# A two-layer transformer block: earlier stack loads, one weight ring for all stages, other bytes for raw weights, later stores

## The chip, the cores and the metric

The kernel runs on one core of a Trainium2 chip. The metric is the device time of one execution in microseconds (us). Five engines work side by side, each through its own instructions in order: PE (TensorE) multiplies matrices, DVE (VectorE) and ACT (ScalarE) do elementwise work, POOL (GpSimd) does elementwise work and issues DMAs, SP (SyncE) issues DMAs only. They wait for each other by semaphores.

## The reference

Two layers over 1024 latent tokens and 256 context tokens of width 1024. Each layer norms and modulates the tokens, projects them, runs four mixers side by side, adds their projected output, and ends in a gated feed-forward. All of it is float32.

```
for l in range(DEPTH):                                  # DEPTH = 2
    need_ctx = l < DEPTH - 1
    u_lat = modulate(rms_norm(h, norm1_g[l]), sh1, sc1)
    u_ctx = modulate(rms_norm(hc, norm1_g[l]), csh1, csc1)
    y_lat, y_ctx = hybrid_mixer(u_lat, u_ctx, ...)      # mLSTM | attention | pooling | convolution
    h = h + g1 * (y_lat @ w_out[l])
    h = h + g2 * swiglu(modulate(rms_norm(h, norm2_g[l]), sh2, sc2), ffn_w_in[l], ffn_w_out[l])
    if need_ctx:
        hc = hc + cg1 * (y_ctx @ w_out[l])
        hc = hc + cg2 * swiglu(modulate(rms_norm(hc, norm2_g[l]), csh2, csc2), ffn_w_in[l], ffn_w_out[l])

def diff_softmax_attend(q, k, v, lam):                  # 4 heads, two maps m each
    s = jnp.einsum('bqhmd,bkhmd->bhmqk', q, k) * (A_HD ** -0.5)
    p = jax.nn.softmax(s, axis=-1)
    a = p[:, :, 0] - lam * p[:, :, 1]
    return jnp.einsum('bhqk,bkhe->bqhe', a, v)

def swiglu(u, w_in, w_out):
    g, up = jnp.split(u @ w_in, 2, axis=-1)
    return (jax.nn.silu(g) * up) @ w_out
```

The mLSTM is a recurrence over chunks of tokens, forward and backward.

## The kernel before

**Precision.** Each float32 operand is split into a high part and a rest (names ending in h and l; ACT copies the high part, DVE or POOL subtracts it), and each product is three matmuls: high by high, low by high, high by low (`mm3`).

**Stages of a layer.** A: norm, projections, mLSTM, convolution, pooling (`mixers`, line 612). B: attention (line 1171). C: output projection `out_proj` and the second norm (`norm_ffn`), lines 1412 and 1454. F: `ffn_in` (line 1536), in Strassen's form: 11 pairs of feature tiles by two halves x (gate, up), so 22 phases; in each, four loaded weights A11 to A22 and four sums S1 to S4 of them (POOL, lines 1552 to 1555) give seven products of 12 matmuls per part of the tokens; in layer 0 the context's products lie between them. G: `ffn_out`. In layer 0 the span is A 0 to 555, B to 870, C to 985, F to 1590, G to 1935; in layer 1 A ends at 2346, B near 2640, C at 2706, F at 3160.

**Memory.** Tiles come from pools with a number of buffers per tag; a new tile waits until the last reader of the buffer's former tile is done. A stage's pools are closed at its end, and the next stage's pools lie on their bytes, with the same kind of wait per tile. U: 16 big tiles that hold the normed projection input (uh, ul, two tiles for each of 8), later attention's stacks. S: 12 tiles of the same size for the mLSTM. The weight ring (`load_w`, line 299: tags wh, wl with 5 buffers, raw wr with 2) belongs to stages A to C; stage F has its own tags fr (raw weights), fh, fl (their split), ft (temporaries), and there the context's h is loaded into fr buffers, too (line 1519).

**Attention's input.** q and k are normed, rotated and written by POOL's queue to a DRAM tensor qks (line 991). `stacks(h)` (line 1184) loads head h from there, again by POOL's queue: for each of two maps m two copies of the rows of Qs and one Ks, into U tiles. The scores sc are matmuls of Ks by Qs.

**Order.** The Tile framework's scheduler places the instructions of each engine by priority in the order written, up to the attention; in attention PE, ACT and DVE are kept in the order written. In the mLSTM's loop the projections of attention's q, k and v and the convolution are interleaved by hand: `nfill` units of the generator `fill` are spread over the loop's 22 steps, and what is left of it runs behind the loop.

```
        steps = 2 * (len(self.oc) + 1)
        nfill = 24 if need else 20
```

Of the kernel before, what the change touches and what calls it, by code (L numbers as in the profile page):

```python
# [18 lines left out]
P = 128  # L19
D = 1024  # L20
KT = 8
# [163 lines left out]
class Builder:  # L185
    def __init__(self, tc, a, ctx):
        self.tc, self.a = tc, a
        self.ordered = False
        self.nc = Ordered(self, tc.nc)
        e = ctx.enter_context  # L190
        self.cp = e(tc.tile_pool(name="cp", bufs=1))
        self.qp = e(tc.tile_pool(name="qp", bufs=12))
        self.ps = None
        self.npool = 0
        self.dp = e(tc.tile_pool(name="dp", bufs=1, space=bass.MemoryType.DRAM))


# [9 lines left out]
    def open_mixers(self):  # L207
        self.mx = ExitStack()
        self.wx = ExitStack()
        self.wp = self.mkpool(self.wx, "right")  # L210
        self.tp = self.mkpool(self.mx, "left")
        self.sp = self.mkpool(self.mx, "left")
        self.mp = self.mkpool(self.mx, "left")
        self.temps = (self.tp, TW, 11)

    def E(self, tag, bufs, dt=F32, n=512):
        return self.fp.tile([P, n], dt, tag=tag, name=tag, bufs=bufs)

    def stage(self, temps=None):

        if self.fx is not None:
            self.fx.close()
        if temps:
            if self.tx is not None:
                self.tx.close()
            self.tx = ExitStack()
            self.temps = (self.mkpool(self.tx, "right"), 512, temps)
        self.fx = ExitStack()
        self.fp = self.mkpool(self.fx, "right")

# [381 lines left out]
    def mixers(self, l, u, norm, early_out):  # L612
# [102 lines left out]
        steps = 2 * (len(self.oc) + 1)  # L715
        nfill = 24 if need else 20
        done = step = 0
# [9 lines left out]
        for c in list(self.oc) + [None]:  # L727
            if old:
                next(old)
            if c is not None:  # L730
                new = self.mlstm_chunk(c, kT, qT, Cst)
                next(new)
            background()
            if old:
                next(old)
            if c is not None:
                next(new)
            background()
            old = new
        for _ in fill:  # L740
            pass
# [363 lines left out]
    def conv(self, acc):  # L1105
# [61 lines left out]
        for _ in range(5):  # L1167
            if next(self.rest):
                yield

    def attention(self, early):

        nc, l = self.nc, self.l
        ident = self.c("ident")
        ya = [self.S(f"ya{i}") for i in range(2)]
        gd = nc.gpsimd.dma_start

        def dup(ap):
            return AP(tensor=ap.tensor, offset=ap.offset, ap=[[0, 2]] + [list(x) for x in ap.ap])
        q0 = 0 if self.need else NCTX  # L1180
        els = [self.mp.tile([P, 2, NCH], F32, name="el", tag="el", bufs=2) for _ in range(2)]
        heads = {}

        def stacks(h):
            Qs, Ks = [], []
            for m in range(2):
                mp = 2 * h + m
                Qm = self.U(f"Qs{m}", F32R)
                for x in range(2):
                    gd(Qm[x * 64:x * 64 + 64, q0:NT].bitcast(F32), dup(self.qk_scr[0, mp, x, :, q0:NT].bitcast(F32)))  # L1190
                Km = self.U(f"Ks{m}", F32R)
                self.stack = gd(Km[:, 0:NT].bitcast(F32),
                                dup(self.qk_scr[1, mp].rearrange("a r n -> (a r) n").bitcast(F32)))
                Qs.append(Qm)
                Ks.append(Km)
            V = self.U("V")[:, :NCH * 64].rearrange("p (c x) -> p c x", x=64)
            nc.sync.dma_start(V, self.v_scr[h])
            heads[h] = (Qs, Ks, V)

        def scores(h, b0, nk, at):  # L1200
# [3 lines left out]
            for qb in range(2):  # L1204
# [3 lines left out]
                sums = (L0, ls[:, 3:4])  # L1208
                pr = [self.S(f"pr{m}") for m in range(2)]
                for m in range(2):  # L1210
# [52 lines left out]
        def values(h, b0, nk, aT):  # L1263
# [4 lines left out]
            for kt in range(nk):  # L1268
# [4 lines left out]
                if kt == nk // 2 - 1:  # L1273
                    yield
            yield
            for b in range(2):
                self.copy(ya[h // 2][rows, b0 + b * P:b0 + (b + 1) * P], po[b * 64:b * 64 + 64, 0:P])
# [65 lines left out]
        for k in range(max(plan) + 1):  # L1343
            if k == 0:
                stacks(0)
            if k % (4 * len(nblk)) == 2 and k // (4 * len(nblk)) < 3:
                stacks(k // (4 * len(nblk)) + 1)
            ev = plan.get(k, [])
# [63 lines left out]
    def out_proj(self, l, src, dst, chunks, later):  # L1412
# [5 lines left out]
        for i, (c0, n) in enumerate(chunks):  # L1418
# [12 lines left out]
            for nt in range(KT):  # L1431
# [7 lines left out]
                nc.vector.scalar_tensor_tensor(hv, ps[:, :n], self.mod[l][:, 16 + nt, v:v + 1], hv, ALU.mult, ALU.add)  # L1439
                nc.sync.dma_start(dst[nt][:, cs], hv)  # L1440
                for _ in range(3):
                    next(todo, None)
                if squares and nt:
                    squares.send(h[nt - 1])
            if i == 0:
                self.ux.close()
# [7 lines left out]
    def norm_ffn(self, l, need):  # L1454
# [58 lines left out]
        def ctx(src):  # L1513

            n = NCTX
            t = [self.E("uc", KT, F32R) for _ in range(KT)]
            h = [self.E("fr", 8)[:, :n] for _ in range(KT)]
            for k in range(KT):
# [17 lines left out]
    def ffn_in(self, l, state, mid, need, side):  # L1536
# [7 lines left out]
        def weights(f, x):  # L1544
            raw = {}
            for i, (ff, pc) in enumerate(((f, 0), (f, 1), (f + 1, 0), (f + 1, 1))):
                raw[i] = self.E("fr", 8 + 3 * more)
                nc.sync.dma_start(raw[i], self.a["ffn_in"][l, ff, x, pc])
            for i in (self.S1, self.S2, self.S3, self.S4):
                raw[i] = self.E("fr", 8 + 3 * more)  # L1550
            A11, A12, A21, A22, S1, S2, S3, S4 = range(8)
            gp(raw[S1], raw[A21], raw[A22], ALU.add)
            gp(raw[S2], raw[S1], raw[A11], ALU.subtract)
            gp(raw[S3], raw[A11], raw[A21], ALU.subtract)
            gp(raw[S4], raw[A12], raw[S2], ALU.subtract)
            return raw

        def split(raw):
            hi, lo = self.E("fh", 5 + 2 * more, F32R), self.E("fl", 5 + 2 * more, F32R)
            self.copy(hi, raw)  # L1560
            self.sub_lo(lo, raw, hi)
            return hi, lo
# [140 lines left out]
    def run(self):  # L1703
        nc, a = self.nc, self.a
        self.fx = self.tx = None
        self.open_u()
# [16 lines left out]
        for l in range(DEPTH):  # L1723
# [8 lines left out]
            self.phase("C")  # L1732
            self.stage(4)
            mid = self.dp.tile([KT, P, NT], F32, name=f"hmid{l}")
            state, norm = self.norm_ffn(l, need)
            self.out_proj(l, src, mid, ch, norm)
            self.phase("F")
            self.fx.close()
            self.tx.close()
            self.wx.close()  # L1740
            self.fx = self.tx = None
# [3 lines left out]
            self.phase("G")  # L1745
            self.stage()
            if need:
# [10 lines left out]
            later = iter(())  # L1758
            self.fx.close()
            self.tx.close()  # L1760
            self.fx = self.tx = None
            if need:
# [83 lines left out]
```

## Time and profile before

| | |
|---|---|
| three runs | 3417.82, 3414.29, 3411.08 us (median 3414.29) |
| the profiled execution | 3415.06 us, its span 3413.3 us |
| PE busy | 3020.0 us, 88% |
| DVE, ACT, POOL busy | 1935.9, 1318.5, 846.8 us |
| mean granted clock of PE | 0.939 of full speed |
| moved by DMA | 393.37 MB |

Times in the profile are microseconds from the span's start. A row of instructions names line, engine, operation, output<-input. All of PE, ACT and DVE stand under line 165, through which a helper records them; so groups are told apart by their tiles: tmps are projections, pS, pi and pN the mLSTM's matmuls, sc attention's scores, ops the output projection, nps a norm's sums, fps the feed-forward's products, fcs the same of the context. A waits row gives what an engine waited for, the sum, how often, and the longest. PEclk is the granted clock, 1.00 for 2.4 GHz and 0.50 for 1.2 GHz.

### The profile page before, as it was taken

Reading aid. Unit: us, or ns where it says so; the run is one execution under the profiler, and the core shown is the slowest. Engines: PE = TensorE matmul, PEld = TensorE weight load, DVE = VectorE, ACT = ScalarE, POOL = GpSimd, SP = SyncE. Lnnn points to the kernel's source line nnn. Section 1 sums busy time; section 2 is a strip of 40 time slices with the busy share of each in tenths; the row PEclk is TensorE's granted clock in tenths of the full one; section 3 lists DMA queues with packets and bytes.
Section 4 is the critical chain, followed back from the end, with each engine's and each line's share of the span. In section 5 each row is a group of like instructions: output and inputs, shape, how many; then the busy total and the mean of one; then the engine's idle time right before and its main releaser. Section 6 shows DMA issues by size and latency. Waiting matters only on the chain. (4 is left out here: it accounts for less than half of the span.)

```text
span 3413.3 us, 44185 instructions
## 1 busy us (share of the span) xinstructions
PE 3020.0 (88%) x16144; PEld 2399.7 (70%) x16144; DVE 1935.9 (57%) x3023; ACT 1318.5 (39%) x2605; POOL 846.8 (25%) x650
## 2 busy tenths in 40 slices
PE   7999885788978999999999798985879699999999
PEld 3767664556656888887887686764656478888787
DVE  6494565884447666763345559554882554544333
ACT  4212444774333222223334522433873433332322
POOL 2240321322223323321000224231322244433000
PEclk9999987988988999999999899987989899999999
DMA  7122334124743333333544411234226323221653
GB/s 269 55 73 98 94 87 97 42 62 167 239 132 115 121 111 118 117 112 116 176 170 165 132 41 47 74 104 87 58 56 237 123 93 98 75 86 50 208 171 134
DMA packets 295578, 393.37 MB, mean 115 GB/s; under 512 B 70720, under 2 KB 140480, under 8 KB 295360
## 3 DMA queue, kind: packets, MB, share of 16 engines
q1 hardware_dynamic: 251392, 360.47, 32.7%
q0 software_dynamic: 43968, 30.07, 4.7%
q8 instruction: 127, 2.08, 0.3%
q14 instruction: 91, 0.75, 0.1%
HBM read 304.28 MB, written 85.98 MB: 114 GB/s over the span
## 5 line engine op out<-in xcount | busy, mean ns | idle before, releaser
L165 PE MATMUL fps<-Uh,fh 128*128 128x512 f32 (+1 forms) x1288 | 495.8, 385 | 51.5 <-ACT fh L165 38.4
L165 PE MATMUL fps<-Uh,fl 128*128 128x512 f32 (+1 forms) x1288 | 493.7, 384 | 0.9 <-DVE fl L165 0.9
L165 PE MATMUL fps<-Ul,fh 128*128 128x512 f32 (+1 forms) x1288 | 494.2, 384 | 0.0
L165 ACT ACTIVATE fh<-fr 128x512 fp32r<-128x512 f32 x330 | 207.1, 631 | 543.7 <-PE fps L165 386.1
L165 DVE TENSOR_TENSOR fl<-fr,fh 128x512 fp32r<-128x512 f32 x330 | 269.7, 819 | 137.0 <-ACT fh L165 131.5
L165 PE MATMUL xps<-gl,xh 128*128 128x512 f32 (+1 forms) x880 | 327.2, 372 | 12.0 <-DVE gl L165 11.8
L165 PE MATMUL xps<-gh,xh 128*128 128x512 f32 (+1 forms) x880 | 327.7, 373 | 9.4 <-ACT xh L165 8.3
L165 PE MATMUL xps<-gh,xl 128*128 128x512 f32 (+1 forms) x880 | 326.1, 372 | 0.3 <-DVE xl L165 0.2
L165 PEld LDWEIGHTS fps<-Uh,fh 128*128 128x128 f32 x1288 | 245.8, 191 | 104.4 <-ACT fh L165 40.0
L165 DVE TENSOR_TENSOR ft<-fps,ft 128x512 f32<-128x512 f32 (+1 forms) x230 | 152.8, 665 | 237.5 <-PE fps L165 233.3
L165 PEld LDWEIGHTS fps<-Uh,fl 128*128 128x128 f32 x1288 | 245.4, 191 | 49.8 <-DVE fl L165 1.9
L165 PEld LDWEIGHTS fps<-Ul,fh 128*128 128x128 f32 x1288 | 245.9, 191 | 43.8 <-issue 0.8
L165 PE MATMUL sc<-Ks,Qs 128*128 128x512 f32 (+1 forms) x400 | 131.9, 439 | 142.5 <-ACT pr L165 84.4
L165 DVE TENSOR_REDUCE ls<-sc 128x1 f32<-128x1280 f32 (+1 forms) x144 | 195.1, 1367 | 80.2 <-PE sc L165 79.8
L165 PE MATMUL fmps<-uh,wfh 128*128 128x512 f32 (+1 forms) x592 | 222.9, 376 | 14.9 <-ACT kT L165 14.9
L165 PE MATMUL fmps<-ul,wfh 128*128 128x512 f32 (+1 forms) x592 | 223.1, 377 | 0.0
L165 ACT ACTIVATE pr<-sc,ls 128x1280 f32<-128x1280 f32 (+1 forms) x144 | 178.4, 1239 | 114.8 <-DVE ls L165 112.6
L165 PE MATMUL fmps<-uh,wfl 128*128 128x512 f32 (+1 forms) x592 | 221.3, 374 | 0.0
L165 DVE TENSOR_TENSOR gl<-gl,gh 128x512 fp32r<-128x512 f32 (+1 forms) x110 | 70.9, 645 | 259.8 <-ACT gh L165 259.7
L165 PEld LDWEIGHTS sc<-Ks,Qs 128*128 128x128 f32 x400 | 76.6, 220 | 176.0 <-ACT pr L165 107.1
L165 DVE SCALAR_TENSOR_TENSOR acc<-cy,par,acc 128x1286 f32<-128x1286 f32 (+28 forms) x120 | 199.4, 1699 | 1.0
L165 PEld LDWEIGHTS xps<-gl,xh 128*128 128x128 f32 x880 | 168.5, 192 | 41.4 <-DVE gl L165 13.3
(305 smaller groups left out, 6342.2 us busy)
## 6 DMA issues: line engine op xcount, KB each, us to landing
xr<-in_ffn_out SPq DMA_DIRECT2D x220, 256.0 KB, 3.3
fr<-in_ffn_in SPq DMA_DIRECT2D x176, 256.0 KB, 2.9
mw<-in_mod_w SPq DMA_DIRECT2D x160, 256.0 KB, 3.1
gs<-ft SPq DMA_DIRECT2D x99, 256.0 KB, 2.5
gl<-gs SPq DMA_DIRECT2D x88, 256.0 KB, 3.3
wfr<-in_w_fm SPq DMA_DIRECT2D x56, 256.0 KB, 2.6
wh<-wos SPq DMA_DIRECT2D x48, 256.0 KB, 3.8
wl<-wos SPq DMA_DIRECT2D x48, 256.0 KB, 4.1
```

The costliest lines, as they stand in the source:

```text
L165: ins = f(*args, **kw)
```

## The change

1. `stacks` becomes a method that takes the kind of tile. For head 0 it is called with S tiles, behind the mLSTM's loop and ahead of the rest of `fill`; V stays where it was (`stack_v`). For head 0 the second probability tile lies in U in return, and ya is made at its first use. `nfill` becomes 18 and 15.
2. The weight ring opens once for the whole kernel, on the left side; stage F's splits use its wh and wl tags (5 buffers) in place of fh and fl (5, in layer 1 seven).
3. Tags named in `etags` get a pool of their own on the right: in C it is yh and yl, in F it is fr; so fr lies on the bytes of yh and yl. fr has 7 buffers for 8 (layer 1: 11 as before). The context's h goes to ft tiles.
4. hmid's tile is stored two steps later. qp has 11 buffers for 12.

```
-        self.qp = e(tc.tile_pool(name="qp", bufs=12))
+        self.qp = e(tc.tile_pool(name="qp", bufs=11))
...
+        self.wp = self.mkpool(ctx, "left")
...
-        self.wx = ExitStack()
-        self.wp = self.mkpool(self.wx, "right")
...
     def E(self, tag, bufs, dt=F32, n=512):
-        return self.fp.tile([P, n], dt, tag=tag, name=tag, bufs=bufs)
+        pool = self.ep if tag in self.etags else self.fp
+        return pool.tile([P, n], dt, tag=tag, name=tag, bufs=bufs)
...
+        self.etags = tags
+        self.ep = self.mkpool(self.fx, "right")
         self.fp = self.mkpool(self.fx, "right")
...
-        nfill = 24 if need else 20
+        nfill = 18 if need else 15
...
+        self.heads = {}
+        self.stacks(0, self.S)
         for _ in fill:
             pass
         self.phase("B")
...
+    def stacks(self, h, new):
+        gd = self.nc.gpsimd.dma_start
...
+        for m in range(2):
+            mp = 2 * h + m
+            Qm, Km = new(f"Qs{m}", F32R), new(f"Ks{m}", F32R)
+            for x in range(2):
+                gd(Qm[x * 64:x * 64 + 64, q0:NT].bitcast(F32), dup(self.qk_scr[0, mp, x, :, q0:NT].bitcast(F32)))
+            gd(Km[:, 0:NT].bitcast(F32), dup(self.qk_scr[1, mp].rearrange("a r n -> (a r) n").bitcast(F32)))
...
-                pr = [self.S(f"pr{m}") for m in range(2)]
+                pr = [(self.U if m and h == 0 else self.S)(f"pr{m}") for m in range(2)]
...
             if k == 0:
-                stacks(0)
+                self.stack_v(0)
             if k % (4 * len(nblk)) == 2 and k // (4 * len(nblk)) < 3:
-                stacks(k // (4 * len(nblk)) + 1)
+                self.stacks(k // (4 * len(nblk)) + 1, self.U)
+                self.stack_v(k // (4 * len(nblk)) + 1)
...
-                nc.sync.dma_start(dst[nt][:, cs], hv)
+                if nt > 1:
+                    nc.sync.dma_start(dst[nt - 2][:, cs], h[nt - 2][:, :n])
...
+            for nt in (KT - 2, KT - 1):
+                nc.sync.dma_start(dst[nt][:, cs], h[nt][:, :n])
...
-            h = [self.E("fr", 8)[:, :n] for _ in range(KT)]
+            t2 = [self.E("ft", 9) for _ in range(KT // 2)]
+            h = [t2[k // 2][:, k % 2 * n:k % 2 * n + n] for k in range(KT)]
...
-                raw[i] = self.E("fr", 8 + 3 * more)
+                raw[i] = self.E("fr", 7 + 4 * more)
...
-            hi, lo = self.E("fh", 5 + 2 * more, F32R), self.E("fl", 5 + 2 * more, F32R)
+            hi, lo = (self.wp.tile([P, 544], F32R, tag=t, name=f"f{t}", bufs=5)[:, :512] for t in ("wh", "wl"))
...
-            self.stage(4)
+            self.stage(4, ("yh", "yl"))
...
-            self.stage(6)
+            self.stage(6, ("fr",))
```

How the instructions move is shown at three places; the numbers in names tell tiles apart and differ between the two kernels.

POOL, layer 0, at the end of the mixers. czl is the low part of the convolution's output, Qs and Ks are the stacks, and x2 behind a row stands for two instructions in a row. Before the change the order is this, with head 0's stacks up to Ks1_4666 and head 1's behind:

```order
L297 TENSOR_TENSOR czl_4077<-acc0_790,czh_4076 128x256
L297 TENSOR_TENSOR czl_4077<-acc1_791,czh_4076 128x256
L297 TENSOR_TENSOR czl_4405<-acc0_790,czh_4404 128x512
L297 TENSOR_TENSOR czl_4405<-acc1_791,czh_4404 128x512
L1190 DMA Qs0_4658<-qks0_430 64x1x1280 x2
L1192 DMA Ks0_4661<-qks0_430 128x1x1280
L1190 DMA Qs1_4663<-qks0_430 64x1x1280 x2
L1192 DMA Ks1_4666<-qks0_430 128x1x1280
L1190 DMA Qs0_4695<-qks0_430 64x1x1280 x2
```

After the change POOL's order is this, with head 0's stacks up to Ks1_4476:

```order
L301 TENSOR_TENSOR czl_4283<-acc0_790,czh_4282 128x256
L1189 DMA Qs0_4470<-qks0_430 64x1x1280
L301 TENSOR_TENSOR czl_4283<-acc1_791,czh_4282 128x256
L1189 DMA Qs0_4470<-qks0_430 64x1x1280
L1190 DMA Ks0_4471<-qks0_430 128x1x1280
L1189 DMA Qs1_4475<-qks0_430 64x1x1280 x2
L1190 DMA Ks1_4476<-qks0_430 128x1x1280
L301 TENSOR_TENSOR czl_4531<-acc0_790,czh_4530 128x512
L301 TENSOR_TENSOR czl_4531<-acc1_791,czh_4530 128x512
L1189 DMA Qs0_4693<-qks0_430 64x1x1280 x2
L1190 DMA Ks0_4694<-qks0_430 128x1x1280
```

The stacks of head 0 now stand between the last czl, ahead of the two of 512 columns; those of head 1 follow these as before.

SP, layer 1, at the end of the output projection: wh and wl are its last weights, hmid the tensor that is stored, fr_22295 to fr_22301 (after: fr_22305 to fr_22311) the first four weights of ffn_in. Before the change the queue is this:

```order
L1394 DMA wh_22146<-wos1_20802 128x512
L1394 DMA wl_22147<-wos1_20802 128x512
L1440 DMA hmid1_21348<-h_21759 128x512
L1440 DMA hmid1_21348<-h_21760 128x512
L1440 DMA hmid1_21348<-h_21761 128x512
L1548 DMA fr_22295<-in_ffn_in 128x512
L1548 DMA fr_22297<-in_ffn_in 128x512
L1548 DMA fr_22299<-in_ffn_in 128x512
L1548 DMA fr_22301<-in_ffn_in 128x512
```

After the change the same stretch of the queue is this:

```order
L1406 DMA wh_22151<-wos1_20806 128x512
L1406 DMA wl_22152<-wos1_20806 128x512
L1453 DMA hmid1_21355<-h_21766 128x512
L1459 DMA hmid1_21355<-h_21767 128x512
L1564 DMA fr_22305<-in_ffn_in 128x512
L1564 DMA fr_22307<-in_ffn_in 128x512
L1459 DMA hmid1_21355<-h_21768 128x512
L1564 DMA fr_22309<-in_ffn_in 128x512
L1564 DMA fr_22311<-in_ffn_in 128x512
L1564 DMA fr_22545<-in_ffn_in 128x512
```

The first two loads of ffn_in now stand ahead of the last store of hmid.

SP, the first weights of layer 1 (wtr, from in_w_vg). hscr is the tensor that layer 0's ffn_out stores, gl and xr are ffn_out's first loads, gs0 is where ffn_in stores. Before the change the four loads stand behind layer 0's last stores:

```order
L1697 DMA hscr_13114<-h_15946 128x256
L1697 DMA hscr_13114<-h_15989 128x256
L1697 DMA hscr_13114<-h_16032 128x256
L1697 DMA hscr_13114<-h_16075 128x256
L304 DMA wtr_16180<-in_w_vg 128x544
L304 DMA wtr_16186<-in_w_vg 128x544
L304 DMA wtr_16192<-in_w_vg 128x544
L304 DMA wtr_16198<-in_w_vg 128x544
L304 DMA wfr_16520<-in_w_fm 128x512
```

After the change the last two of them stand here, at the end of ffn_in of layer 0:

```order
L1564 DMA fr_12908<-in_ffn_in 128x512
L1684 DMA gl_13135<-gs0_7981 128x512
L1692 DMA xr_13137<-in_ffn_out 128x512
L308 DMA wtr_16196<-in_w_vg 128x544
L1659 DMA gs0_7981<-ft_12721 128x4x128
L1659 DMA gs0_7981<-ft_12724 128x4x128
L308 DMA wtr_16202<-in_w_vg 128x544
L1659 DMA gs0_7981<-ft_12722 128x4x128
L308 DMA wfr_16524<-in_w_fm 128x512
L308 DMA wfr_16530<-in_w_fm 128x512
```

The last two of the four loads, and the first wfr behind them, moved from behind ffn_out to among ffn_in's last stores; the first two, wtr_16184 and wtr_16190, stand still further ahead, among the output projection's weights of layer 0.

## Rows read from the trace of the kernel before

**Rows 1.** The page's busy table: busy us, share of the span, instructions

```profile
PE 3020.0 (88%) x16144; PEld 2399.7 (70%) x16144; DVE 1935.9 (57%) x3023; ACT 1318.5 (39%) x2605; POOL 846.8 (25%) x650
```

**Rows 2.** Windows: us, busy (count) PE, PEld, DVE, ACT, POOL; PEclk, DMA share, GB/s

```profile
516.00:532.00 16.00, 15.98 (x131) 13.97 (x131) 10.53 (x28) 6.91 (x20) 0.00 (x0) 1.00 0.19 44
556.00:581.00 25.00, 0.00 (x0) 0.00 (x0) 1.87 (x3) 0.07 (x1) 1.43 (x2) 0.56 0.99 160
581.00:600.00 19.00, 11.48 (x25) 7.08 (x26) 16.19 (x20) 11.64 (x19) 4.32 (x3) 0.50 0.30 84
640.00:826.00 186.00, 147.34 (x1122) 111.96 (x1118) 134.61 (x217) 129.50 (x276) 48.71 (x27) 0.84 0.29 79
985.00:1100.00 115.00, 91.18 (x489) 76.07 (x490) 67.67 (x101) 36.84 (x67) 28.92 (x19) 0.90 0.32 101
1100.00:1590.00 490.00, 486.14 (x2568) 410.32 (x2568) 317.72 (x433) 136.87 (x224) 149.20 (x101) 1.00 0.35 107
2346.00:2376.00 30.00, 0.28 (x3) 0.09 (x2) 0.64 (x1) 0.38 (x1) 4.95 (x8) 0.58 0.90 138
2709.00:2747.00 38.00, 9.19 (x38) 8.37 (x39) 26.42 (x50) 19.91 (x45) 23.01 (x18) 0.51 0.18 62
2745.00:3160.00 415.00, 415.00 (x1895) 346.75 (x1895) 205.17 (x275) 131.81 (x220) 161.55 (x115) 1.00 0.27 79
```

**Rows 3.** Waits of PE, 345 to 556, then 400 to 640: total us, times, longest

```profile
PE pN L165 <- DVE W L165: 7.7, 3, 4.8
PE sc L165 <- DMA Ks<-qks: 26.9, 2, 25.9
```

**Rows 4.** Waits of PE, 2340 to 2400

```profile
PE sc L165 <- DMA Ks<-qks: 30.7, 2, 29.7
```

**Rows 5.** Timeline of POOL, 545 to 560: start, duration, instruction

```profile
548.74 1.36 POOL L1190 DMA_DIRECT2D Qs<-qks  x2 [8.28 <-PE tmps L165]
552.12 0.84 POOL L1192 DMA_DIRECT2D Ks<-qks  x1
```

**Rows 6.** Tile pS, 400 to 556, then whole: min/median/max ns, first and last start

```profile
L165 PE MATMUL pS<-qT,kT x56: 272/272/579, 413.4 to 529.2; 64*128 64x128 f32 x56
L165 PE MATMUL pS<-qT,kT x144: 272/272/579, 345.0 to 2316.0; 64*128 64x128 f32 x144
```

**Rows 7.** DMA issues, 640 to 826: number, KB each, median us to landing

```profile
Qs<-qks POOLq DMA_DIRECT2D x4, 320.0 KB, 21.9
Ks<-qks POOLq DMA_DIRECT2D x2, 640.0 KB, 26.1
```

**Rows 8.** Waits of PE, 2706 to 2745

```profile
PE fps L165 <- ACT fh L165: 31.4, 2, 29.3
```

**Rows 9.** Timeline of SP's queue, 2715 to 2740

```profile
2731.97 3.18 SPq L1548 DMA_DIRECT2D fr<-in_ffn_in  x7
```

**Rows 10.** Timeline of POOL, 2715 to 2745

```profile
2725.11 8.20 POOL L1488 TENSOR_TENSOR Ul<-h,Uh 128x256 fp32r<-128x256 f32 x4 [2.09 <-ACT Uh L165]
2737.40 1.27 POOL L1552 TENSOR_TENSOR fr<-fr 128x512 f32<-128x512 f32 x1 [4.09 <-DMA fr<-in_ffn_in]
```

**Rows 11.** Waits of PE, 985 to 1100

```profile
PE fps L165 <- DVE ft L165: 9.3, 5, 6.7
PE fps L165 <- ACT fh L165: 7.0, 2, 4.5
PE fcs L165 <- ACT uc L165: 5.0, 1, 5.0
```

**Rows 12.** Timeline of SP's queue, 985 to 1036

```profile
995.39 27.65 SPq L1519 DMA_DIRECT2D fr<-hmid  x8
1032.89 2.71 SPq L1548 DMA_DIRECT2D fr<-in_ffn_in  x4
```

**Rows 13.** Waits of PE, 1930 to 1960

```profile
PE tmps L165 <- ACT wth L165: 12.0, 1, 12.0
```

**Rows 14.** Timeline of SP's queue, 1930 to 1955

```profile
1943.59 6.39 SPq L304 DMA_DIRECT2D wtr<-in_w_vg  x4
```

More of the change, by code (lines that the diff above doesn't have):

```diff
@@ L216, in E, with end_stage, stage @@
     def E(self, tag, bufs, dt=F32, n=512):
-        return self.fp.tile([P, n], dt, tag=tag, name=tag, bufs=bufs)
-    def stage(self, temps=None):
-        if self.fx is not None:
-            self.fx.close()
+        pool = self.ep if tag in self.etags else self.fp
+        return pool.tile([P, n], dt, tag=tag, name=tag, bufs=bufs)
+    def end_stage(self, temps=True):
+        self.fx.close()
         if temps:
-            if self.tx is not None:
-                self.tx.close()
+            self.tx.close()
+    def stage(self, temps=None, tags=()):
+        if temps:
             self.tx = ExitStack()
@@ L1169, in conv, with dup, stack_v @@
                 yield
+    def stacks(self, h, new):
+        gd = self.nc.gpsimd.dma_start
+        def dup(ap):
+            return AP(tensor=ap.tensor, offset=ap.offset, ap=[[0, 2]] + [list(x) for x in ap.ap])
+        q0 = 0 if self.need else NCTX
+        Qs, Ks = [], []
+        for m in range(2):
[4 more added lines that the diff above has]
+            gd(Km[:, 0:NT].bitcast(F32), dup(self.qk_scr[1, mp].rearrange("a r n -> (a r) n").bitcast(F32)))
+            Qs.append(Qm)
+            Ks.append(Km)
+        self.heads[h] = [Qs, Ks, None]
+    def stack_v(self, h):
+        V = self.U("V")[:, :NCH * 64].rearrange("p (c x) -> p c x", x=64)
+        self.nc.sync.dma_start(V, self.v_scr[h])
+        self.heads[h][2] = V
     def attention(self, early):
@@ L1174, in attention @@
         ident = self.c("ident")
[L1175 to L1179, printed above, removed]
+        ya = {}
         q0 = 0 if self.need else NCTX
         els = [self.mp.tile([P, 2, NCH], F32, name="el", tag="el", bufs=2) for _ in range(2)]
[L1182 to L1198, printed above, removed]
+        heads = self.heads
         def scores(h, b0, nk, at):
@@ L1275, in values @@
             yield
+            if h // 2 not in ya:
+                ya[h // 2] = self.S(f"ya{h // 2}")
             for b in range(2):
@@ L1546, in weights @@
             for i, (ff, pc) in enumerate(((f, 0), (f, 1), (f + 1, 0), (f + 1, 1))):
-                raw[i] = self.E("fr", 8 + 3 * more)
+                raw[i] = self.E("fr", 7 + 4 * more)
                 nc.sync.dma_start(raw[i], self.a["ffn_in"][l, ff, x, pc])
             for i in (self.S1, self.S2, self.S3, self.S4):
-                raw[i] = self.E("fr", 8 + 3 * more)
+                raw[i] = self.E("fr", 7 + 4 * more)
             A11, A12, A21, A22, S1, S2, S3, S4 = range(8)
@@ L1704, in run @@
         nc, a = self.nc, self.a
-        self.fx = self.tx = None
         self.open_u()
@@ L1737, in run @@
             self.phase("F")
[L1738 to L1741, printed above, removed]
-            self.stage(6)
+            self.end_stage()
+            self.stage(6, ("fr",))
             self.ffn_in(l, state, mid, need, self.mod_vec(l + 1) if need else iter(()))
@@ L1745, in run @@
             self.phase("G")
+            self.end_stage(False)
             self.stage()
@@ L1758, in run @@
             later = iter(())
-            self.fx.close()
-            self.tx.close()
-            self.fx = self.tx = None
+            self.end_stage()
             if need:
```

## The prediction

> **What bounds the kernel now.** I read the page's busy table first: the matmul engine PE is busy 3020.0 us, 88% of a span of 3413.3 us [rows 1]. So the sum of all other work matters only where PE stands still, and a change that adds and removes no arithmetic can win only out of the remaining 393 us. Next I cut the span into its stages with the windows view [rows 2]. The long feed-forward stretches are full: PE idles 3.9 us of 490 in the stretch from 1100 in layer 0, and not at all in the stretch from 2745 in layer 1. The idle time lies at the seams: 25 us from 556 with PE at 0.00, 30 us from 2346 with 0.28, 29 of the 38 us from 2709, 24 of the 115 us from 985. Each is paid for a second time, since PE comes back at a granted clock of 0.50 or 0.51, its lower level. Last I asked the waits view who ends each of these, then the queue that the releaser came through. Four seams carry the answer.
>
> **The two attention starts.** The first scores wait 25.9 us in layer 0 for the stack Ks [rows 3] and 29.7 us in layer 1 [rows 4]. That is a DMA on POOL's queue, first issued at 548.74 [rows 5], some 7 us before the gap, because its U tile holds the projections' input until nearly the last projection has read it. While PE waits, DVE is busy 1.87 us of 25 and the DMA engines 0.99 of the time at 160 GB/s [rows 2]: the gap is pure transfer. After the change the six transfers of head 0 go to S tiles, whose last reader is the mLSTM. In the new order of POOL they wait for the last pS and pi matmuls of the last chunk instead of the last tmps. The row on pS dates that: its last matmul of layer 0 starts at 529.2, of layer 1 at 2316.0 [rows 6], some 26 and 30 us before the gaps. In the new order more stands behind it, because the mLSTM loop takes 18 (layer 1: 15) instead of 24 (20) units of fill. I count 165 tmps matmuls there in layer 0 and 188 in layer 1; at 15.98 us for 131 matmuls [rows 2] that is 20 and 23 us, and the convolution's matmuls and the last chunk's pN bring the cover to about 35 and 38 us (my estimate). The need: four Qs of 320 KB and two Ks of 640 KB [rows 7] are 2.62 MB, 16.4 us at 160 GB/s, behind 4.2 us of issue (548.74 to 552.96 [rows 5]): 21 us. The slower value is 26.1 us, which a Ks of a later head took [rows 7]. Both are under the cover, so the wait goes: 25.9 + 29.7 = 55.6 us, of which I leave 2 for a tail. What is late next is DVE, busy 16.19 of the first 19 us of attention [rows 2]; so the better clock there brings little, 2 us for both layers (0 to 6).
>
> One rule of the Trainium skill speaks against this move. The rows first: in the gap of before, DVE is nearly idle while POOL issues and the data moves, but in the place where the stacks go now DVE is busy 10.53 of 16 us [rows 2]. The page "SBUF — State Buffer" (sections "SBUF: two separate sides" and "Who interferes with whom") says that descriptors of a DMA issued from POOL are written by GpSimd, and that a VectorE instruction in a two-port mode locks it out, so that such a DMA starves beside a busy VectorE. By that rule the stacks would take up to three times as long as in the gap. The trace does not bear it out: the stacks of a later head, issued in the stretch from 640, where DVE is busy 134.61 of 186 us, landed after medians of 21.9 and 26.1 us [rows 7].
>
> **The price of the thinner loop.** Six units of fill in layer 0 and five in layer 1 leave the loop; a full one is 24 matmuls, 24 x 0.122 = 2.9 us, so up to 17.6 and 14.6 us of PE work no longer cover the recurrence. Lower bound of the cost 0, if the loop has slack; upper bound all of it, 32 us, if the loop's length is set by its own chain. In the stretch from 516 PE is busy 15.98 of 16 us, DVE 10.53 [rows 2], which speaks for slack; the recurrence itself is waited for only 7.7 us in layer 0 (pN on DVE's W [rows 3]). I take a doubling of that row in half: 4 us per layer, 8 in all, near the lower end.
>
> **From the output projection to the feed-forward, layer 1.** PE waits 29.3 us for the first fh [rows 8]. The chain behind it: fr's bytes are those of the h tiles, POOL's last four Ul end at 2725.11 + 8.20 = 2733.3, the first weight load is issued at 2731.97 [rows 9, 10]. Then S1 to S4 begin at 2737.40, and 38 matmuls run at half clock up to 2747 [rows 2]. After the change fr lies on the bytes of yh and yl, free with the last ops, and the loads stand ahead of the last hmid store. A11, S2 and S3 need only the halves of the first tokens that are split early, so three products (36 matmuls) run inside the norm chain. The S1 product stands on ACT behind all Uh of the chain, so PE resumes where the chain ends: 2733.3 plus about 2 us for the splits and POOL sums that now stand ahead of the chain, 2735, in the state that it has at 2747 now. That is 12 us. Off goes the clock: the first 38 matmuls took 9.19 us there for the half clock, about half of it, 4.6, lost, and that is paid after 2735 now: 12 - 4.6 = 7.4 us (4 if the chain is drawn out by the early sums, 14 if the clock holds).
>
> **The start of the feed-forward, layer 0.** In the stretch from 985 PE idles 24 us; the waits are 9.3 for DVE's ft, 7.0 for fh, 5.0 for uc [rows 11]. The cause is on SP: eight loads of context h into fr buffers go out over 27.65 us, and the next weights are issued only at 1032.89 [rows 12]. Now the context's h has ft tiles of its own, so the loads follow at once and the next weights are bound by fr buffers alone. The first weight load moves ahead by one store only. Fewer buffers (7 for 8) and a norm that PE meets earlier give some back. Between 4 and 16 of the 21.3 us of those three waits, I take half, 10.
>
> **From layer 0 to layer 1.** PE waits 12.0 us for wth [rows 13]; its load is issued at 1943.59 [rows 14], as the weight ring's bytes belong to the last stage until then. With a ring that stays open, the four w_vg loads stand in the out_proj and ffn_in part of SP's queue, and the first two chunks of tmps follow the norm directly. The third still waits for the gate tiles' memset behind the norm on POOL. I take 11 (8 to 14).
>
> **At nothing.** The ffn's splits move into the ring of five (layer 1 had seven) and its raw buffers are 7 for 8 and 11 for 11: hidden by the full PE of both steady stretches, and the price if that cover is gone is a rival below. Stores of hmid two steps later, so that SP isn't held by them: 0 to 2 us gained; but nps now follows the last ops closer, with h work behind it: 0 to 3 lost; together -1. qp with 11 buffers, ya made late, one pr in U: 0 to 3 lost, I take 1.
>
> **The sum.** 55.6 - 2 + 2 - 8 + 7.4 + 10 + 11 - 1 - 1 = 74.0 us. The profiled execution took 3415.06 us, its span 3413.3 and 1.8 around it; 3415.06 - 74.0 = 3341.1. The median of the runs shown is 0.8 lower, 3414.29, so I predict 3340 us.
>
> **The rivals.** (1) The loop lives off the fill. Then most of the 32 us come back, say 24 more than the 8 taken: 3364. For it: the three waits of pN; against it: PE's 15.98 of 16. (2) The stacks starve or are held on POOL. If they moved only while DVE is free, a third of the time, 16.4 us become 48, with issue 52, and against 35 to 38 of cover PE waits 17 and 14 us: 55.6 shrinks to 25 and the sum to 44: 3370. By the Trainium skill's page named above this is what would happen; rows 7 speak against it. (3) Slower: the ring of five binds the feed-forward. Every product's hi and lo wait for the slot of the product five earlier, and ACT's and DVE's splits queue behind that wait, in 22 phases of each layer. From 1.7 us a phase on (74 / 44) the whole gain is gone; at 2 us it costs 88 us: 3428. For it: layer 1 loses two of seven slots. Against it: layer 0 ran on five already, with 3.9 us of idle time in 490 [rows 2]. (4) The stacks don't come early at all, since something else on POOL's or SP's queue ahead of them is late: 55.6 stays, the rest holds: 3395. (5) More: the loop costs nothing, the clock is full at both attention starts and the two feed-forward starts give 16 and 14: 3340 - 8 - 4 - 12.6 = 3315.
>
> **How the numbers follow.** Chances: the forecast 0.57, rival 1 0.14, 2 0.08, 3 0.05, 4 0.04, 5 0.12. The forecast's own bounds (the starts 8 and 16, the loop a few us either way) make it 3322 to 3359. For 8 in 10 the range takes in rival 5 and rivals 1 and 2: 3312 to 3375. Within 0.2%, about what a measurement can tell from no change, is 7 us either side; only rival 3 near its turning point falls there: 0.03. Slower 0.04, faster 0.93.
>
> **What would show it.** Right: in the waits of PE the row sc <- DMA Ks is under 5 us in each layer, and POOL's first Qs issue lies 30 us or more ahead of the first sc; after the last ops of layer 1 three products of fps stand inside the norm chain, and the next group starts at its end; no 12 us wait for wth; SP's weight loads of the second phase of layer 0 lie right behind the context loads. Wrong: pN <- W grows by more than 8 us a layer, sc still waits for a DMA, or PE idles in the steady feed-forward stretches on fwh or fwl.

## The result and the profile after

The changed kernel takes 3368.34 us (median of four runs, 3358.72 to 3377.49) against 3412.68 us (four runs, 3407.45 to 3417.82): a ratio of 0.987, 95% interval 0.9837 to 0.9902. It is faster by 44 us, where 74 were forecast. The profiled execution is the shortest of its four, 3358.72 us, 56 us under the one of before; so the places below add up to some 12 us more than the medians.

The page's first lines of the changed kernel; the columns are those of [rows 1]:

```profile
span 3356.9 us, 44207 instructions
PE 3027.0 (90%) x16144; PEld 2395.0 (71%) x16144; DVE 1938.1 (58%) x3023; ACT 1316.6 (39%) x2602; POOL 842.0 (25%) x650
```

PE has the same 16144 matmuls as in [rows 1], but they are busy 7 us longer. I come back to that. To see where the time went I took in both traces the start of the same matmul at each seam (of the last ops its end) and subtracted. Times are us from the span's start.

| first or last of its kind | before | after | after less before | gained in this stretch | forecast |
|---|---|---|---|---|---|
| first sc, layer 0 | 581.2 | 563.4 | -17.9 | 17.9 | 21.9 |
| end of the last ops, layer 0 | 984.6 | 960.2 | -24.4 | 6.5 | -1 |
| 337th fps, layer 0 | 1101.1 | 1051.7 | -49.4 | 25.0 | 10 |
| last fps, layer 0 | 1592.5 | 1548.0 | -44.6 | -4.8 | 0 |
| last xps, layer 0 | 1931.1 | 1889.5 | -41.6 | -3.0 | 0 |
| first tmps, layer 1 | 1946.9 | 1893.0 | -53.9 | 12.4 | 11 |
| first pS, layer 1 | 2166.0 | 2114.6 | -51.4 | -2.6 | 0 |
| first sc, layer 1 | 2376.0 | 2308.0 | -68.0 | 16.6 | 25.7 |
| end of the last ops, layer 1 | 2701.8 | 2633.1 | -68.7 | 0.7 | 0 |
| 169th fps, layer 1 | 2762.6 | 2690.0 | -72.7 | 4.0 | 7.4 |
| last fps, layer 1 | 3162.3 | 3099.8 | -62.5 | -10.2 | 0 |
| end | 3413.3 | 3356.9 | -56.4 | -6.1 | 0 |

(The forecast at an attention start is the wait that goes, less 1 us of tail and 4 of the loop, plus 1 for the clock; one of the two single microseconds that the prediction takes off has no row of its own.) Three entries are far off: the second attention start, the feed-forward's start in layer 0, and the losses in the steady feed-forward, where the forecast had nothing. Two smaller ones were not forecast either. Of the 6.5 us up to the last ops of layer 0, 3.6 are shorter waits of the output projection for its stored weights, 12.0 us in place of 15.6. The 6.1 us lost at the end belong to this one execution as far as is known: the changed kernel again (e1) takes 254.7 us there and e4, one of the experiments below, 251.8, against 257.1 here and 251.0 before.

**The attention starts.** Waits of PE around both, the first two rows from 345 to 560, the last from 2250 to 2310; they answer to [rows 3, 4]:

```profile
PE pt L165 <- DVE hs L165: 14.1, 7, 7.5
PE pN L165 <- DVE W L165: 4.5, 3, 2.2
PE sc L165 <- DMA Ks<-qks: 13.3, 1, 13.3
```

In layer 0 Ks is no longer waited for there, but a new one has come: pt, which transposes the mLSTM's result hs, waits 14.1 us for DVE. The thin loop ends before the last chunks' own chain does. In layer 1 Ks is still waited for 13.3 us. POOL's timeline there (start, duration, line, instruction, and the idle time before it) answers to [rows 5]:

```profile
2279.94 1.08 POOL L301 TENSOR_TENSOR czl<-acc,czh 128x512 fp32r<-128x512 f32 x1 [37.09 <-ACT czh L165]
2280.97 0.69 POOL L1189 DMA_DIRECT2D Qs<-qks  x1
2283.43 0.79 POOL L1190 DMA_DIRECT2D Ks<-qks  x1
2285.47 0.82 POOL L1190 DMA_DIRECT2D Ks<-qks  x1
```

The last of the stacks' tiles was free with the last pS at 2252, but the first Qs stands behind a czl, before which POOL stood idle for 37.09 us until ACT had its czh. So the transfer starts at 2281, not at 2252. The transfer itself is no slower than before; the tile view's line on Ks, over all its loads (the median of before is 24.2, too), and the window up to the first sc (columns as in [rows 2]):

```profile
DMA to landing us min/median/max: 19.7/24.2/26.6
```

```profile
2252.00:2308.00 56.00, 38.86 (x258) 32.59 (x258) 22.01 (x48) 20.27 (x48) 9.04 (x12) 0.90 0.48 104
2281.00:2308.00 27.00, 13.72 (x75) 10.39 (x75) 3.42 (x5) 4.76 (x10) 7.99 (x12) 0.82 0.78 161
```

DVE is busy 22.01 us of the 56, but only 3.42 of the 27 in which the data move.

**The feed-forward's starts.** In layer 0 the waits of 21 us [rows 11] are nearly gone; waits from 960 to 1076, and SP's queue, which answers to [rows 12]:

```profile
PE nps L165 <- ACT nsq L165: 3.4, 1, 3.4
PE fps L165 <- ACT fwh L165: 1.3, 2, 0.9
PE fcs L165 <- DVE uc L165: 0.7, 2, 0.5
```

```profile
962.64 3.70 SPq L1535 DMA_DIRECT2D ft<-hmid  x8
971.21 6.03 SPq L1564 DMA_DIRECT2D fr<-in_ffn_in  x3
977.81 1.70 SPq L1564 DMA_DIRECT2D fr<-in_ffn_in  x1
```

The eight context loads take 3.70 us of the queue instead of 27.65, and the next weights go out from 971 on. In layer 1 the rows of PE with an idle time in the brackets, from 2636 to 2675:

```profile
2641.33 0.58 PE L165 MATMUL fps<-Uh,fwh 128*128 128x256 f32 x1 [2.32 <-ACT fwh L165]
2650.81 0.58 PE L165 MATMUL fps<-Uh,fwl 128*128 128x256 f32 x1 [7.02 <-DVE fwl L165]
2666.34 0.58 PE L165 MATMUL fps<-Uh,fwh 128*128 128x256 f32 x1 [11.09 <-ACT fwh L165]
2671.13 0.58 PE L165 MATMUL fps<-Uh,fwh 128*128 128x256 f32 x1 [3.99 <-ACT ft L165]
```

The three early products ran inside the norm chain, and PE resumed at 2666.3. Shifted back by the 68.7 us gained until there, that is 2735.0, as forecast. But the next product waits 3.99 us for ft, which ACT writes behind the chain's Uh; so 4.0 us are left of 7.4.

**From layer 0 to layer 1** the wait for wth is 5.2 us for Z now, in place of 12.0 [rows 13]:

```profile
PE tmps L165 <- DVE Z L165: 5.2, 1, 5.2
```

**The steady feed-forward.** Windows of 300 us in layer 1, the kernel before and then the changed one (columns as in [rows 2]):

```profile
2850.00:3150.00 300.00, 300.00 (x1325) 248.48 (x1324) 146.20 (x196) 95.64 (x157) 114.32 (x81) 1.00 0.27 78
```

```profile
2790.00:3090.00 300.00, 300.00 (x1292) 243.46 (x1291) 133.21 (x191) 94.57 (x155) 107.71 (x78) 1.00 0.26 75
```

PE is busy 300.00 of 300 us in both, and its clock is 1.00 in both. But 1325 matmuls fit before and 1292 after: 300 us over the count is 226.4 ns against 232.2 (from one start to the next the traces have 226.7 and 232.5). This is the loss of 10 us in layer 1, and no column on busy time shows it.

### The profile page after: what moved, and what is told of

The parts are those of the page before. It is cut to its first block, busy times and chain, and to the rows that moved or that the text cites. A ratio compares the mean times of both kernels' runs of the same rounds, so it can differ in the third digit from the quotient of the medians.

```text
span 3356.9 us, 44207 instructions
## 1 busy us (share of the span) xinstructions
PE 3027.0 (90%) x16144; PEld 2395.0 (71%) x16144; DVE 1938.1 (58%) x3023; ACT 1316.6 (39%) x2602; POOL 842.0 (25%) x650
## 5 line engine op out<-in xcount | busy, mean ns | idle before, releaser
L165 PE MATMUL fps<-Uh,fwh 128*128 128x512 f32 (+1 forms) x1288 | 497.6, 387 | 22.5 <-ACT fwh L165 15.5
L165 PE MATMUL fps<-Uh,fwl 128*128 128x512 f32 (+1 forms) x1288 | 500.8, 390 | 7.7 <-DVE fwl L165 7.7
L165 PE MATMUL fps<-Ul,fwh 128*128 128x512 f32 (+1 forms) x1288 | 499.2, 388 | 0.0
L165 ACT ACTIVATE fwh<-fr 128x512 fp32r<-128x512 f32 x330 | 207.8, 631 | 545.3 <-PE fps L165 400.3
L165 DVE TENSOR_TENSOR fwl<-fr,fwh 128x512 fp32r<-128x512 f32 x330 | 256.6, 779 | 134.0 <-ACT fwh L165 130.6
L165 PEld LDWEIGHTS fps<-Uh,fwh 128*128 128x128 f32 x1288 | 246.8, 192 | 79.6 <-ACT fwh L165 17.8
L165 PEld LDWEIGHTS fps<-Uh,fwl 128*128 128x128 f32 x1288 | 243.7, 190 | 60.2 <-DVE fwl L165 9.3
L165 PEld LDWEIGHTS fps<-Ul,fwh 128*128 128x128 f32 x1288 | 244.8, 190 | 49.5 <-issue 0.2
L165 PEld LDWEIGHTS xps<-gh,xh 128*128 128x128 f32 x880 | 168.7, 192 | 47.8 <-ACT xh L165 10.5
```

The source lines that it names most:

```text
L165: ins = f(*args, **kw)
```

## The experiments

Each was timed beside the kernel before on the same chip; where two experiments ran on different chips, their ratios to it are compared. They are called e1 to e11 in the order of the record. **The changed kernel again**, as a baseline for the others:

> The changed kernel itself, timed again beside the others of this call, since its four runs lie between 3358.7 and 3377.5 us. Expected: about 3365 us, a ratio to before of 0.983 to 0.990. In its trace as in the first: PE waits 10 to 15 us for Ks at the second attention start and under 3 us at the first, and the 512-column products of layer 1's steady feed-forward start 232 ns apart, where the kernel before has 226.7.

Measured (e1): 3370.65 us, ratio 0.9871 (0.9848 to 0.9893). Ks is waited for 17.2 us in layer 1, above the 10 to 15 expected, pt for hs 24.5 us in all. The gain is 44.8 us.

**The weight ring in pairs.**

```
-        hi = self.wp.tile([P, 544], F32R, tag="wh", name=f"{nm}h", bufs=5)
-        lo = self.wp.tile([P, 544], F32R, tag="wl", name=f"{nm}l", bufs=5)
+        at = 512 if n <= 512 else 544
+        t = self.wp.tile([P, 1088], F32R, tag="w", name=nm, bufs=5)
+        hi, lo = t[:, :n], t[:, at:at + n]
```

(the same in `out_w` and in the feed-forward's `split`)

> The weight ring's high and low part lie in one tile of 1088 words, five of them, the same bytes in all; so each part of 512 columns starts at the same offset modulo 256 bytes, where the ring of 544-word tiles alternates between two. Theory (the start of the weight tiles sets the pace of the matmuls): the interval in layer 1's steady feed-forward falls from 232.5 to about 227 ns, 1848 x 5.5 ns = 10 us in layer 1 and some 5 us in layer 0; time 12 to 16 us below e1. Rival (it is the ring's place beside the U tiles, or the moved DMAs): the interval stays at 232 ns, time within 4 us of e1.

Measured (e2): 3344.99 us, ratio 0.979 (0.9768 to 0.9811), 25.7 us below e1. The window of 300 us:

```profile
2780.00:3080.00 300.00, 300.00 (x1326) 248.47 (x1325) 152.71 (x198) 97.02 (x159) 117.89 (x83) 1.00 0.27 78
```

1326 matmuls, where the kernel before has 1325. The mechanism held, the size was above the range. In the profiled executions the steady feed-forward of layer 1 gives 10 us. Layer 0's gives nothing: its matmuls come faster, too, but those that start over 300 ns behind the one before went from 48 to 63, and from 21 to 31 us in sum, perhaps because high and low part now come free together. So the pace of the feed-forward accounts for less than half of the 25.7 us, and the rest was not taken apart.

The same trace limits the rule. The projections fmps have their weights from the same paired ring, and they stay at 231.9 ns in layer 0 and 232.2 in layer 1, against 231.5 and 230.2 in the changed kernel; the output projection's ops come down only from 232.1 and 232.4 ns to 230.2 and 230.4 (512 columns, means of the starts under 300 ns apart). So equal starts of the weights are not enough everywhere. The tokens that the fmps multiply lie in U tiles, whose size, 1304 words, lets their starts vary as well; whether that is the reason was not tried.

**The same cause put into the kernel before.**

```
-            hi, lo = self.E("fh", 5 + 2 * more, F32R), self.E("fl", 5 + 2 * more, F32R)
+            hi, lo = self.E("fh", 5 + 2 * more, F32R, 544)[:, :512], self.E("fl", 5 + 2 * more, F32R)
```

> The kernel before, with one edit: the feed-forward's fh tiles (high part of the weights) are 544 words apart instead of 512, the fl tiles stay; nothing else moves. Theory (weight tiles that start at different offsets modulo 256 bytes slow the matmuls, wherever they lie): the products of layer 1's steady feed-forward, 226.7 ns apart in the kernel before, come 229 to 233 ns apart, and the time is 5 to 12 us above before. Rival (it was the ring's neighbourhood to the U tiles): 226.7 ns as before, time within 3 us of before.

Measured (e5): 3430.3 us, ratio 1.0037 (1.0025 to 1.0049), that is 13 us slower than before by the ratio and just above the range; the window:

```profile
2860.00:3160.00 300.00, 300.00 (x1301) 244.17 (x1300) 138.76 (x193) 94.97 (x156) 111.60 (x80) 1.00 0.26 78
```

300 / 1301 = 230.6 ns, far from the U tiles; nothing else changed but that the tiles behind fh in their pool start a little later. So it is where the weight tiles start, not what lies near them.

The trace says which starts. In layer 1, where fh has seven buffers, the products repeat with period seven: three run at 226.8 ns, as before, and four at 232.9 to 233.4. In layer 0, with five buffers, two of five run at 227.8, as before, and three at 232.8 to 233.3. If fl lies behind fh, three of seven and two of five are just the products whose fh and fl start at the same offset modulo 256 bytes (worked out from the sizes of the tiles; the traces hold no addresses). By the same working the two parts differ in every product of the changed kernel, and all of them are slow there, 231.1 to 234.2 ns in layer 1. So what slows a product of the feed-forward is that its high and its low part start at different offsets, not a bad offset and not the step from one product to the next. Whether the boundary that counts is 256 bytes or another was not tried.

**Head 0's stacks through SP.**

```
-        gd = self.nc.gpsimd.dma_start
+        gd = (self.nc.gpsimd if h else self.nc.sync).dma_start
```

> Head 0's stacks are issued by SP instead of POOL, all else as in the changed kernel. Theory (the 13 us wait of layer 1 comes from POOL's order: the first Qs stands behind a czl that waits until 2280 for ACT, while its tile is free at 2253): the stacks are issued some 20 us earlier, the wait for Ks in layer 1 falls from 13.3 to under 2 us, layer 0's stays under 3; time 9 to 14 us below e1. Rival (the transfer is slow there because other work starves it or its tile is freed late): issued earlier, landed no earlier, the wait stays above 8 us.

Measured (e3): 3423.83 us, ratio 1.0024 (1.0010 to 1.0038): the whole gain is gone, and neither theory had that. SP's queue around the stacks of layer 1, and waits of PE from 505 to 600:

```profile
2318.96 1.11 SPq L1189 DMA_DIRECT2D Qs<-qks  x2
2320.16 0.48 SPq L1190 DMA_DIRECT2D Ks<-qks  x1
2320.73 8.85 SPq L1189 DMA_DIRECT2D Qs<-qks  x2
2329.67 18.20 SPq L1190 DMA_DIRECT2D Ks<-qks  x1
2347.96 13.96 SPq L1166 DMA_DIRECT2D ys<-yct  x1
```

```profile
PE cvar L165 <- ACT csq L165: 22.2, 2, 21.2
PE pt L165 <- DVE hs L165: 19.9, 2, 19.1
```

The first two Qs and the first Ks cost SP 1.11 and 0.48 us, but the next two Qs take 8.85 and the second Ks 18.20, where POOL took 1.36 and 0.84 [rows 5]. What stands behind them on SP waits: the stores of avt among them. ACT, whose next csq needs avt's buffer, stops, and PE waits for csq and hs. In layer 1 the first Qs still goes out 27 us behind the last pS, and Ks is waited for twice, 41.5 us in sum. So the stacks did not go out earlier, and the run says nothing on POOL's order, which it was made for.

**The stacks written earlier.**

```
         for c in list(self.oc) + [None]:
+            if c is None:
+                self.heads = {}
+                self.stacks(0, self.S)
             if old:
```

(on top of e2, and without the call behind the loop)

> The kernel of e2 with the stacks of head 0 written into the program at the start of the loop's last step, so that POOL issues them ahead of the last two czl in layer 1 (in layer 0 between them as before). Theory (in layer 1 POOL's order delays them by some 25 us): first Qs of layer 1 issued 15 us or more earlier than 2281, Ks is no longer waited for over 4 us, time 8 to 14 us below e2 (3345), about 3334. Rival (the transfer is slowed by other work in the queues, as in e3): the wait stays above 8 us and the time within 4 us of e2.

Measured (e8): 3347.67 us, ratio 0.9799 (0.9779 to 0.9818): as e2. There is no row for Ks any more, but the time did not move. POOL's rows, and PE's wait for hs over the whole span:

```profile
2225.63 0.67 POOL L1195 DMA_DIRECT2D Qs<-qks  x1 [7.75 <-DMA qks<-qr]
2235.26 0.68 POOL L1195 DMA_DIRECT2D Qs<-qks  x1
2263.24 0.80 POOL L1196 DMA_DIRECT2D Ks<-qks  x1 [12.83 <-PE pS L165]
```

```profile
PE pt L165 <- DVE hs L165: 26.4, 10, 9.7
```

The stacks now stand on POOL ahead of the last rotations' work and hold that instead: the last pS of layer 1 comes 8.8 us later than in e2, and the first sc 0.7 us earlier.

**POOL's order without either.**

```
-                self.sub_lo(zz[i][1], vs[i], zz[i][0], None if last else nc.gpsimd)
+                self.sub_lo(zz[i][1], vs[i], zz[i][0])
```

(on top of e2: DVE computes every czl)

> The kernel of e2 with the convolution's czl computed by DVE, so that nothing stands between the last qks write and head 0's stacks on POOL, and nothing earlier on POOL is held either. Theory (e8 removed the wait for Ks but put stacks that wait in front of the projections' work on POOL): Qs of layer 1 issued at the last pS, some 25 us earlier than in e2, no wait for Ks over 4 us in layer 1, the last pS not later than in e2, time 6 to 13 us below e2 (3345): 3332 to 3339. Rival (DVE, which now waits for czh in its own order, hands the wait on to hs and the rotations): pt <- hs over 25 us, time within 4 us of e2 or above.

Measured (e9): 3331.76 us, ratio 0.977 (0.9752 to 0.9789). By the ratio this is 7 us below e2, though the intervals overlap. POOL's rows, and the wait for hs over the whole span:

```profile
2245.31 1.34 POOL L1194 DMA_DIRECT2D Qs<-qks  x2
2254.38 0.78 POOL L1195 DMA_DIRECT2D Ks<-qks  x1 [7.74 <-PE pS L165]
2256.42 0.81 POOL L1195 DMA_DIRECT2D Ks<-qks  x1
```

```profile
PE pt L165 <- DVE hs L165: 9.5, 8, 2.8
```

The first Qs are issued at 2245 and Ks at 2254.38, with the last pS (2254.0); Ks is not waited for, and hs only 9.5 us. With e8, where the stacks go ahead of the czl and Ks is not waited for either, this shows that POOL's order caused the 13 us wait. But the wait is not worth its length: the first sc of layer 1 comes 3.8 us earlier only, as PE has some 40 us of its own work behind the loop, and it waits for csq, avt and hs in between. The wait for hs in layer 0 fell, too, from 16.2 us in e2 to 2.6.

**The fuller loop.**

```
-        nfill = 18 if need else 15
+        nfill = 24 if need else 20
```

> The mLSTM loop takes 24 (layer 1: 20) units of fill again instead of 18 (15), all else as in the changed kernel. Theory (the thinner loop and the earlier end of the loop cost about 8 us a layer, in waits of PE for hs of the last chunks): the wait pt <- hs falls from 21.7 to under 8 us in all, but fewer matmuls cover the stacks, and the wait for Ks grows to 15 to 25 us in layer 1 and to 5 to 12 in layer 0; time from 5 us below to 15 above e1. Rival (the fill was not needed in the loop): pN <- W and pt <- hs stay as they are, and the time rises by the whole uncovered transfer, 15 to 25 us.

Measured (e4): 3365.81 us, ratio 0.9847 (0.9826 to 0.9867), so its interval overlaps e1's. The wait for hs fell to 7.9 us as expected; the wait for Ks did not grow but vanished, against both theories, while other rows grew:

```profile
PE cvar L165 <- ACT csq L165: 18.4, 4, 11.7
PE pN L165 <- DVE W L165: 13.5, 4, 3.8
PE pt L165 <- DVE hs L165: 7.9, 7, 3.9
```

In layer 1 the last pS comes 24 us later than in e1, at 2280.7 (half of that stood already at the first pS), but the czl ahead of the stacks runs at 2289.7: the first Qs goes out at 2290.8, 10 us behind the last pS and 30 us ahead of the first sc. In the changed kernel's first trace it was 29 us behind the one and 27 ahead of the other. On top of e9:

> As e9, with nfill 24 and 20 again. Theory (with the stacks issued at once, the 26 to 30 us of work that the fuller loop leaves behind it cover nearly all of the transfer, and the loop's waits for hs go): pt <- hs under 8 us in all, the wait for Ks 0 to 6 us in each layer, time 0 to 8 us below e9. Rival (the cover is too short): Ks is waited for 8 us or more in each layer, time at or above e9.

Measured (e10): 3332.34 us, ratio 0.9777 (0.9756 to 0.9798): no difference to e9. pt waits 13.2 us for hs, not under 8, and Ks nowhere. In layer 0 the first sc came 13 us later than in e9, in layer 1 9 us earlier. Taken apart by layer:

> As e9 and e10, with nfill 18 in layer 0 and 20 in layer 1. In the traces of those two, layer 0 reaches its first scores earlier with 18 (557.7 against 570.8) and layer 1's mLSTM and the rest take 13 us less from its first projection to its first scores with 20. Theory (the two stages are independent): first scores of layer 0 near 558, from the first pS of layer 1 to its first sc 183 us as in e10, time 5 to 12 us below e9 and e10 (3332). Rival (the difference between layers is scatter of single executions, as the equal medians of e9 and e10 suggest): within 4 us of both.

Measured (e11): 3329.95 us, ratio 0.975 (0.9724 to 0.9776), the fastest of all and faster than both kernels. Its first sc of layer 0 is at 558.9, and from the first pS to the first sc of layer 1 it takes 183.8 us, as expected; by the ratios it is 7 us below e9, in overlapping intervals.

**The context's h alone, in the kernel before.**

```
-            h = [self.E("fr", 8)[:, :n] for _ in range(KT)]
+            t2 = [self.E("ft", 9) for _ in range(KT // 2)]
+            h = [t2[k // 2][:, k % 2 * n:k % 2 * n + n] for k in range(KT)]
```

> The kernel before, with one edit: the context's h of the feed-forward's norm is loaded into ft tiles instead of fr. Theory (the eight context loads that wait for fr buffers hold SP's queue and so the next weights; this alone made the start of layer 0's feed-forward 25 us faster): the wait rows of the stretch 985 to 1100 (21 us in all) fall under 6, and the time is 15 to 25 us below before. Rival (the gain came from fr's new bytes and the moved stores): under 8 us below before.

Measured (e6): 3389.64 us, ratio 0.9925 (0.9910 to 0.9941), 25 us below before, from this edit of three lines. Waits from 960 to 1080:

```profile
PE fps L165 <- ACT fh L165: 5.0, 2, 4.4
PE fcs L165 <- DVE uc L165: 1.0, 1, 1.0
PE fps L165 <- DVE ft L165: 0.9, 1, 0.9
```

The 21 us of [rows 11] are down to 6.9 (under 6 were expected), and the granted clock, 0.90 from 985 to 1100 in [rows 2], is 0.94 from 980 to 1072 here.

**The change without its stacks.**

```
-        nfill = 18 if need else 15
+        nfill = 24 if need else 20
...
-        self.stacks(0, self.S)
...
             if k == 0:
+                self.stacks(0, self.U)
                 self.stack_v(0)
```

> The changed kernel without its first part: head 0's stacks go to U tiles at the start of attention again, nfill 24 and 20, both probability tiles in S. Theory (the stacks' part is worth 18 to 20 us at layer 0's attention start and 15 to 17 at layer 1's): time 32 to 40 us above the changed kernel's (3365 to 3371), some 3400 to 3408, and the waits for Ks are 24 to 31 us in each layer again. Rival (the scheduler gives part of it elsewhere, since the rest of fill then runs later): under 25 us above.

Measured (e7): 3390.4 us, ratio 0.9917 (0.9902 to 0.9933). Waits over the whole span:

```profile
PE sc L165 <- DMA Ks<-qks: 55.2, 4, 27.5
PE pt L165 <- DVE hs L165: 1.7, 3, 0.9
```

The waits for Ks are back, 55.2 us in all, and hs costs nothing. Yet the kernel is only 20 us slower than e1 (22 than the median above), below the range of the theory. In the traces the stacks' part gains 20 us at the first sc of layer 0; from the first pS to the first sc of layer 1 it gains 13 us against the changed kernel's first trace and 9 against e1's.

## Why the prediction was right

The direction and each place were right, and the time lies in the range. But the gain came out 30 us under the forecast's 74, and 3368 lies outside the forecast's own bounds, 3322 to 3359. The range held because it took in rivals 1 and 2, and neither of them happened as written: the loop did not give back 32 us, and nothing starved. Some luck was in it, too, as errors of both signs met: the feed-forward's start in layer 0 gave 15 us more than forecast, the ring took 15 that had no term. Two of the prediction's own signs failed in layer 1: sc still waits for Ks (13.3 us), and the first Qs goes out 27 us ahead of the first sc, not 30 (45 in layer 0).

- **The stacks, 55.6 us.** This is the term that was mis-sized. The waits did go, 25.9 to nothing and 29.7 to 13.3, but the part is worth 20 us by e7's time and 29 to 33 by the traces, not 48 with its tail, loop and clock. Two steps failed. "In the new order of POOL they wait for the last pS and pi matmuls" left out that POOL works in order: in layer 1 a czl stands in front. The prediction's own piece of the order showed that czl ahead of Qs for layer 0. That is rival 2's "held on POOL", or rival 4's late work ahead of them, in one layer and without the starving. And a cover of 35 us is worth its length only if PE is not held while it covers.
- **The thinner loop, 8 us.** Right in kind, in another row: not pN but pt waited, 21.7 us in all against 1.7, and pN's wait fell from 15.9 to 5.2. In sum about 9 us of waits. In time the fuller loop (e4) differs from e1 by 5 us, in overlapping intervals; e11 suggests that the thin loop helps layer 0 and hurts layer 1.
- **The feed-forward's start in layer 0, 10 us.** Too low. I took half of the waits for fear of the other parts; of the 21.3 us under 3 are left, and the clock rose from 0.90 to 0.94 (960 to 1052). e6 shows that one edit did it.
- **Layer 0 to layer 1, 11 us**: right, 12.4 in the trace.
- **C to F of layer 1, 7.4 us**: 4.0. PE resumed where forecast, and then ACT was late with ft.
- **"At nothing", the ring in the feed-forward.** The rows read it as hidden, since PE is full there. PE waited for no slot, so rival 3 was wrong; but a full PE ran 2.5% slower there, because in the ring of 544-word tiles high and low part of a weight start at different offsets. This cost some 15 us: 10.2 in layer 1 and 4.8 in layer 0 by the first trace, and 13 where e5 put a milder form of it into the kernel before. (e2, which undid it, gained 25.7, but only 9 of that lie in the feed-forward of its trace.) With these 15 the forecast would have been 74 - 15 = 59.
- **The rule that speaks against the move** (the Trainium skill, "SBUF — State Buffer", section "Who interferes with whom": a DMA that POOL issues starves while a DVE instruction in a two-port mode runs) did not show here: Ks landed after a median of 24.2 us. It was hardly put to the test, though. While the data moved, DVE was busy 8.44 of 24 us in layer 0 (521 to 545) and 3.42 of 27 in layer 1, less than the 10.53 of 16 that the prediction had in mind, and the traces do not tell which instructions ran in such a mode.

## What to carry to other kernels

Full is not the same as fast: before costing a move of a busy engine's operands at nothing, count its instructions per 100 us, not only its busy share. When a transfer is to start earlier, read what stands ahead of it on the queue that issues it, and what that waits for; a free buffer is only one of two conditions. And look first for the small edit, for here three lines on the context's h, put into the kernel before, gave 25 us, where the whole change gave 44.

## What the hardware showed that was not expected

- In the steady feed-forward, matmuls of 512 columns that alternate between the high and the low part of a weight started 226.7 ns apart when both parts start at the same offset modulo 256 bytes, and 231.1 to 234.2 ns apart when the two offsets differ by 128 bytes (before, after, e2, e5; the offsets worked out from tile sizes). The projections stayed near 232 ns with equal starts of their weights, too (e2).
- The same stacks that POOL issues in 0.84 us (Ks) and 1.36 us (two Qs) held SP for up to 18.20 and 8.85 us, and everything behind them on SP, once others were under way (e3; the first ones took 0.48 and 1.11 us). Why SP is held was not tried.
